# Five of the retention's value projections moved from the recurrences into the RWKV projections

## The chip, the cores and the metric

The kernel runs on one core of a Trainium2 chip. The metric is the device time of one execution in microseconds; several executions are taken and their median is the number that is compared.

## The reference, cut to what matters

One decoder block on 1024 tokens of width 1024, in float32. The normalised input goes through one wide projection whose columns feed two token mixers (RWKV-7 and a chunked retention) and two gates; the mixers' outputs are merged, projected, normalised, and a gated convolutional FFN follows.

```python
hn = rms_norm(h, norm_mix_pre[l])
p = hn @ w_in[l]
p_rw, p_ret, g_rw, g_ret = _split(p, IN_SIZES)
y_rw = rwkv7_mixer(p_rw, ...)
y_ret = retention_mixer(p_ret, positions)      # q, k (rotated), v, g; chunks of 128 tokens
merged = (jax.nn.sigmoid(g_rw) * (y_rw @ w_branch_rw[l])
          + jax.nn.sigmoid(g_ret) * (y_ret @ w_branch_ret[l]))
h = h + rms_norm(merged @ w_out[l], norm_mix_post[l])
f = conv_ffn(rms_norm(h, norm_ffn_pre[l]), ...)
h = h + rms_norm(f, norm_ffn_post[l])
```

## The kernel before

Everything is kept transposed: 128 channels on the partitions, tokens along the free axis. The columns of `w_in` are 54 tiles of 128: tiles 0 to 13 are the RWKV projections, 14 to 21 the retention's queries and keys, 22 to 29 its values, 30 to 37 its gate, 38 to 53 the two merge gates. A float32 product is made of three float32r products (`mm3`, lines 199 to 201: high by high, high by low, low by high), so a tile of 128 columns costs, for each half of 512 tokens, 8 times 3 matmuls of 512 columns: 24 rows on PE. `load_w` (line 178) fetches a weight tile on SP's queue, casts the high part on ACT (line 188) and subtracts the low part on DVE or POOL in turn (line 193).

The stages that matter, in the order of the code:

- **RWKV projections** (`rw_tiles`, line 316, and the loop `for i in range(4)`, line 379). Four tiles first, then for each i the decay and rate products `p_lw` and `p_a`, a long chain on DVE, ACT and POOL that makes the recurrence's operands, and the k, r and v tiles of that i. Their product tiles are called `ps_rw`; `p_sb` are the head sums.
- **RWKV recurrence** (line 553), eight chunks.
- **Side tiles**: `qk_pair` (line 481) and `side_tile` (line 509). A side tile projects one of the tiles 22 to 53, copies it out of PSUM (`ps_side`, two buffers of pool psA, shared with `ps_rw` and `ps_b0`) into `ot`, and writes it to the HBM array `pj_d` on ACT's queue. They stand in the code behind the recurrence (lines 741 to 744) and behind the retention (line 849).
- **Retention** (`first_stage` line 754, `second_stage` line 801), eight chunks. A chunk's data `zvg` comes from `pj_d` in one transfer of 1.5 MB into one of two buffers; a buffer is free again when the chunk's last operation, `yr` (line 840), has read it. First stage: transposes `p_v`, `p_k`, products `p_s`, and `vt`, `sm`, the state `R`. Second stage: `p_o`, its statistics (`rst`, `rmv`), an inverse square root of 14 small DVE operations ending in `nb`, eight activations `on` on ACT, transposes `p_y`, the product `yr`, a write to `yret_d`.
- **Merge**: `ps_b0` (line 871), eight products of 12 rows that need the recurrence's output alone, each taken out of PSUM by a DVE operation on `gt0` (line 873); then the products with the retention's output, whose operand is loaded (`yt`, line 950, ACT's queue), cast (`y_hi`, line 955) and subtracted (`y_lo`, line 956).

The order on each engine isn't the code's: a scheduler places every instruction by a simulated timeline, earlier code having priority, so that work that stands behind fills what it takes for gaps. At run time each engine goes through its list in order.

Of the kernel before, what the change touches and what calls it, by code (L numbers as in the profile page):

```python
# [9 lines left out]
F32 = mybir.dt.float32  # L10
# [8 lines left out]
T = 1024  # L19
# [125 lines left out]
def body(tc, nc, xT, xN, pos, wch, wbrw, wbret, wout, wup, wdn, w2a2, gw2, rows, vecs, consts0, consts1, out):  # L145
    V, S, G, PE = nc.vector, nc.scalar, nc.gpsimd, nc.tensor
    ctx = ExitStack()
    with ctx:
# [147 lines left out]


# [5 lines left out]
        with pctx, tc.tile_pool(name="p1", bufs=1, reuse_waits="tile", side="right") as p1:  # L303
# [57 lines left out]
            rt, rg, k0, r0 = rw_tiles([(12, "v_"), (13, "cs"), (4, "k_"), (0, "r_")], w0)  # L361
            nc.sync.dma_start(cst[1], consts1)
# [16 lines left out]
            for i in range(4):  # L379
# [58 lines left out]
                for c in range(2):  # L438

                    o = 2048 + 128 * i + 64 * (1 - c)  # L440
                    nc.scalar.dma_start(L_d[:, :, o:o + 64].rearrange("j p t -> p j t"), v_.rearrange(jct, c=2, t=64)[:, :, c, :])

# [34 lines left out]


        pj_d = dp.tile([40, 128, T], F32, name="pj_d")

        def qk_pair(m):

            ws = [load_w(wch[14 + 2 * m + e], 8) for e in range(2)]
            for hf in range(2):
                h_ = slice(hf * 512, (hf + 1) * 512)
                ab = []
                for e in range(2):
                    ps = psA.tile([128, 512], F32, tag="a", name="ps_side")
                    proj(ws[e], ps, hf)
                    with tc.high_priority(offset=WPRIO):  # L490
                        t = gp.tile([128, 512], F32, tag=f"qk{e}", name="qk", bufs=1)
                        S.copy(t, ps)
                    ab.append(t)
                a_, b_ = ab
                o1 = gp.tile([128, 512], F32, tag="ot", name="ot")
                t2 = gp.tile([128, 512], F32, tag="rt", name="rot", bufs=1)
                G.tensor_tensor(out=o1, in0=a_, in1=cosT[:, h_], op=ALU.mult)
                V.tensor_tensor(out=t2, in0=b_, in1=sinT[:, h_], op=ALU.mult)
                V.tensor_tensor(out=o1, in0=o1, in1=t2, op=ALU.subtract)
                G.tensor_tensor(out=a_, in0=a_, in1=sinT[:, h_], op=ALU.mult)  # L500
                V.tensor_tensor(out=b_, in0=b_, in1=cosT[:, h_], op=ALU.mult)
                o2 = gp.tile([128, 512], F32, tag="ot", name="ot")
                V.tensor_tensor(out=o2, in0=b_, in1=a_, op=ALU.add)
                dst = pj_d[2 * m:2 * m + 2, :, h_].rearrange("i (e z d) t -> z (i e) d t", e=2, z=2)
                for z, o in enumerate((o1, o2)):
                    for n in range(4):
                        nc.scalar.dma_start(dst[z, n], o[32 * n:32 * n + 32, :])

        def side_tile(i):

            w = load_w(wch[i], 8)
            for hf in range(2):
                ps = psA.tile([128, 512], F32, tag="a", name="ps_side")
                proj(w, ps, hf)
                with tc.high_priority(offset=WPRIO):
                    ot = gp.tile([128, 512], F32, tag="ot", name="ot")
                    if i < 30:
                        S.copy(ot, ps)
                    elif i < 38:
                        V.tensor_tensor(out=ps, in0=ps, in1=rbh(hf), op=ALU.mult)  # L520
                        S.activation(ot, ps, AF.Tanh, scale=0.5)
# [221 lines left out]
        for i in range(22, 38):  # L743
            side_tile(i)
# [535 lines left out]
```

## Time and profile before

| | us |
|---|---|
| three runs | 1914.69, 1915.49, 1908.49 (median 1914.69) |
| the profiled execution | 1908.72 |
| its span, first to last instruction | 1906.9 |
| PE busy in the span | 1802.6 |
| DVE busy in the span | 1194.9 |

The rows further down come from the profiled execution. Times are from the span's start; PE is the matmul engine, PEld its weight loads, DVE, ACT and POOL the elementwise engines, SP the engine that only issues transfers. A row of the timeline has start, length, engine, line, operation, tiles and count, and in brackets how long the engine stood idle before it and what ended that. Granted clock is a share of 2.4 GHz; it has two levels, 1.00 and 0.50, and a value between is a mix of them over the stretch.

### The profile page before, as it was taken

What the parts mean: (1) busy time and instruction counts of PE and PEld (TensorE: products, weight loads), DVE (VectorE), ACT (ScalarE), POOL (GpSimd) and SP (SyncE); (2) the same over time, 40 slices, a digit from 0 to 9 for tenths busy, and PEclk for the clock granted to TensorE, in tenths of its full rate; (3) what the DMA queues carried; (4) which work ended last, traced back from release to release, by engine and by line L of the source; (5) the groups of instructions that cost most, each with busy time, mean ns of one, the idle gap of its engine ahead of it and who ended that gap; (6) DMA issues with size and microseconds to landing.
All of it is one profiled execution on the core that took longest, in us unless ns stands there. A gap on an engine that the chain in (4) does not pass through costs nothing.

```text
span 1906.9 us, 27401 instructions
## 1 busy us (share of the span) xinstructions
PE 1802.6 (95%) x10610; PEld 1450.0 (76%) x10610; DVE 1194.9 (63%) x2052; ACT 648.3 (34%) x993; POOL 700.6 (37%) x506
## 2 busy tenths in 40 slices
PE   8779999999999999999999999888999999999996
PEld 7657778788777788878788777666777777777885
DVE  4786585755666635662545728879888887753413
ACT  6543212111111122332343334543444444543320
POOL 1344523312212221011564734745455455223523
PEclk9989999999999999999999999899999999999998
DMA  8333632433333226554653726343222222774531
GB/s 287 92 105 100 191 82 67 133 90 102 101 105 99 73 93 184 148 169 153 227 155 122 246 80 198 127 139 99 81 75 78 78 78 78 223 212 144 180 92 44
DMA packets 202690, 244.44 MB, mean 128 GB/s; under 512 B 60992, under 2 KB 136256, under 8 KB 201536
## 3 DMA queue, kind: packets, MB, share of 16 engines
q1 hardware_dynamic: 125712, 171.11, 29.7%
q10 hardware_dynamic: 76848, 71.59, 11.5%
q8 instruction: 83, 1.36, 0.3%
q14 instruction: 47, 0.39, 0.1%
HBM read 177.10 MB, written 65.54 MB: 127 GB/s over the span
## 4 chain that ended last, share of the span: by engine, by line
PE 48%; DVE 17%; DMA 9%; issue 4%; POOL 3%; ACT 3%; ACTq 0%; SPq 0%; DVEq 0%; POOLq 0%
PE ps_side L199 6%; PE ps_side L200 6%; PE ps_side L201 6%; DVE u_f L1036 4%; PE ps_dn L201 3%; PE ps_dn L200 3%; PE ps_dn L199 3%; POOL w_lo L1130 2%; DMA w_st<-in_wup_dram 2%; DVE u_f L1038 2%; DVE w_sa L1134 2%; DVE w_sa L1133 2%; PE ps_o L200 1%; PE ps_o L201 1%; PE ps_o L199 1%
## 5 line engine op out<-in xcount | busy, mean ns | idle before, releaser
L193 POOL TENSOR_TENSOR w_lo<-w_st,w_hi 128x1024 fp32r<-128x1024 f32 (+2 forms) x107 | 253.4, 2369 | 495.5 <-PE ps_side L201 167.0
L188 ACT CAST w_hi<-w_st 128x1024 fp32r<-128x1024 f32 (+2 forms) x162 | 161.6, 998 | 406.4 <-PE ps_side L200 129.6
L200 PE MATMUL ps_side<-hnl,w_hi 128*128 128x512 f32 x640 | 255.8, 400 | 0.0
L199 PE MATMUL ps_side<-hnh,w_hi 128*128 128x512 f32 x640 | 255.2, 399 | 0.0
L201 PE MATMUL ps_side<-hnh,w_lo 128*128 128x512 f32 x640 | 254.5, 398 | 0.0
L199 PEld LDWEIGHTS ps_side<-hnh,w_hi 128*128 128x128 f32 x640 | 120.8, 189 | 26.8 <-issue 1.5
L200 PEld LDWEIGHTS ps_side<-hnl,w_hi 128*128 128x128 f32 x640 | 120.7, 189 | 26.3 <-issue 1.5
L201 PEld LDWEIGHTS ps_side<-hnh,w_lo 128*128 128x128 f32 x640 | 120.8, 189 | 26.1 <-issue 0.8
L193 DVE TENSOR_TENSOR w_lo<-w_st,w_hi 128x1024 fp32r<-128x1024 f32 (+1 forms) x55 | 72.2, 1313 | 87.3 <-ACT w_hi L188 50.2
L1036 DVE SCALAR_TENSOR_TENSOR u_f<-ub,vct,u_f 128x512 f32<-128x512 f32 x88 | 104.1, 1187 | 10.0 <-ACT u_f L1035 9.9
L1130 POOL TENSOR_TENSOR w_lo<-w_st,w_hi 128x512 fp32r<-128x512 f32 (+1 forms) x53 | 106.2, 2029 | 0.1
L1035 ACT ACTIVATE u_f<-ub,vct 128x512 f32<-128x512 f32 x76 | 60.0, 813 | 124.0 <-DVE ub L1168 102.4
L199 PE MATMUL ps_rw<-hnh,w_hi 128*128 128x512 f32 (+1 forms) x224 | 87.3, 390 | 13.3 <-ACT hnh L264 7.3
L200 PE MATMUL ps_rw<-hnl,w_hi 128*128 128x512 f32 (+1 forms) x224 | 86.3, 385 | 0.1
L201 PE MATMUL ps_rw<-hnh,w_lo 128*128 128x512 f32 (+1 forms) x208 | 79.9, 384 | 0.0
L201 PE MATMUL ps_b<-y_hi,w_lo 128*128 128x512 f32 x192 | 76.3, 398 | 2.8 <-DVE w_lo L193 2.1
L199 PE MATMUL ps_b<-y_hi,w_hi 128*128 128x512 f32 x192 | 76.2, 397 | 0.9 <-ACT w_hi L188 0.9
L200 PE MATMUL ps_b<-y_lo,w_hi 128*128 128x512 f32 x192 | 76.0, 396 | 0.0
L201 PE MATMUL ps_dn<-f_k,w_lo 128*128 128x512 f32 (+1 forms) x198 | 73.0, 369 | 0.0
L199 PE MATMUL ps_dn<-f_k,w_hi 128*128 128x512 f32 (+1 forms) x198 | 72.9, 368 | 0.0
L200 PE MATMUL ps_dn<-f_k,w_hi 128*128 128x512 f32 (+1 forms) x198 | 72.7, 368 | 0.0
L1038 DVE SCALAR_TENSOR_TENSOR u_f<-ub,vct,u_f 128x512 f32<-128x512 f32 x88 | 71.7, 832 | 0.2
(418 smaller groups left out, 4387.2 us busy)
## 6 DMA issues: line engine op xcount, KB each, us to landing
w_st<-in_wup_dram SPq DMA_DIRECT2D x54, 512.0 KB, 3.6
w_st<-in_wch_dram SPq DMA_DIRECT2D x52, 512.0 KB, 4.0
w_st<-in_wdn_dram SPq DMA_DIRECT2D x38, 512.0 KB, 4.2
pj_d<-ot ACTq DMA_DIRECT2D x64, 256.0 KB, 2.2
zvg<-pj_d SPq DMA_DIRECT2D x8, 1536.0 KB, 9.3
f_d<-u_f ACTq DMA_DIRECT2D x44, 256.0 KB, 2.1
L<-L_d SPq DMA_DIRECT2D x8, 1344.0 KB, 5.9
gt<-pj_d SPq DMA_DIRECT2D x32, 256.0 KB, 4.3
```

The costliest lines, as they stand in the source:

```text
L188: S.copy(hi, st)
L193: eng.tensor_tensor(out=lo, in0=st, in1=hi, op=ALU.subtract)
L199: PE.matmul(ps, wh, xh, start=first and a == 0, stop=False, skip_group_check=skip)
L200: PE.matmul(ps, wh, xl, start=False, stop=False, skip_group_check=skip)
L201: PE.matmul(ps, wl, xh, start=False, stop=last and a == n - 1, skip_group_check=skip)
L1035: S.activation(u, src, AF.Identity, bias=VC("cb")[:, i:i + 1], scale=VC("cw2")[:, i:i + 1])
L1036: V.scalar_tensor_tensor(out=u, in0=ub[:, 1:513], scalar=VC("cw1")[:, i:i + 1], in1=u, op0=ALU.mult, op1=ALU.add)
L1038: V.scalar_tensor_tensor(out=u, in0=ub[:, 0:512], scalar=VC("cw0")[:, i:i + 1], in1=u, op0=ALU.mult, op1=ALU.add)
L1130: eng.tensor_tensor(out=w[1][:, ks, :], in0=src, in1=w[0][:, ks, :], op=ALU.subtract)
L1133: V.tensor_tensor(out=sa[:, lh, :], in0=st2[:, lh, :], in1=st2[:, rh_, :], op=ALU.add)
L1134: V.tensor_tensor(out=sa[:, rh_, :], in0=st1[:, lh, :], in1=st2[:, lh, :], op=ALU.subtract)
```

## The change

`qk_pair`, `side_tile` and the array `pj_d` are moved up in the code, unchanged. Side tiles 22 and 23 are called right behind the first four RWKV tiles, and tiles 24, 25 and 26 at the end of the iterations i = 0, 1 and 2 of the projection loop. The call behind the recurrence begins at tile 27. No operation is added or taken away.

```diff
+        pj_d = dp.tile([40, 128, T], F32, name="pj_d")
+        def qk_pair(m):
...
+        def side_tile(i):
+            w = load_w(wch[i], 8)
+            for hf in range(2):
+                ps = psA.tile([128, 512], F32, tag="a", name="ps_side")
+                proj(w, ps, hf)
+                with tc.high_priority(offset=WPRIO):
+                    ot = gp.tile([128, 512], F32, tag="ot", name="ot")
+                    if i < 30:
+                        S.copy(ot, ps)
...
+                    nc.scalar.dma_start(pj_d[i - 14, :, hf * 512:(hf + 1) * 512], ot)
...
             rt, rg, k0, r0 = rw_tiles([(12, "v_"), (13, "cs"), (4, "k_"), (0, "r_")], w0)
+
+            for i in range(22, 24):
+                side_tile(i)
             nc.sync.dma_start(cst[1], consts1)
...
                     nc.scalar.dma_start(L_d[:, :, o:o + 64].rearrange("j p t -> p j t"), v_.rearrange(jct, c=2, t=64)[:, :, c, :])
+                if i < 3:
+                    side_tile(24 + i)
...
-        for i in range(22, 38):
+        for i in range(27, 38):
             side_tile(i)
```

On PE in the RWKV projections, around the first products with the decay weights (`p_a`, `p_lw`), before:

```order
L201 MATMUL ps_rw<-hnh_0_106,w_lo 128x512
L391 MATMUL p_a<-LA,wlh 128x512
L392 MATMUL p_a<-LA,wll 128x512
L387 MATMUL p_lw<-LW,wlh 128x512
L388 MATMUL p_lw<-LW,wll 128x512
L199 MATMUL ps_rw<-hnh_1_80,w_hi 128x512
```

and now:

```order
L201 MATMUL ps_side<-hnh_0_106,w_lo 128x512
L444 MATMUL p_a<-LA,wlh 128x512
L445 MATMUL p_a<-LA,wll 128x512
L440 MATMUL p_lw<-LW,wlh 128x512
L441 MATMUL p_lw<-LW,wll 128x512
L199 MATMUL ps_side<-hnh_1_80,w_hi 128x512
```

Where rows of the v tile (`ps_rw`) stood, the first side tile stands; in all, 240 side rows now stand among the 568 rows that the projections have behind their first seven half tiles.

On PE at the retention's last chunk (`p_y` are its last transposes), before:

```order
L199 MATMUL ps_side<-hnh_0_82,w_hi 128x512
L839 MATMUL p_y<-cst_69,on 128x128 x2
L200 MATMUL ps_side<-hnl_0_83,w_hi 128x512
L839 MATMUL p_y<-cst_69,on 128x128
L201 MATMUL ps_side<-hnh_0_82,w_lo 128x512
L839 MATMUL p_y<-cst_69,on 128x128 x2
L199 MATMUL ps_side<-hnh_0_86,w_hi 128x512
```

and now, with the rows of the last two chunks:

```order
L796 MATMUL p_R<-vt,kt__6912 64x128 x8
L821 MATMUL p_o<-vt,sm 128x128
L773 MATMUL p_v<-cst_69,zvg 128x128 x4
L782 MATMUL p_s<-zvg 128x128 x8
L773 MATMUL p_v<-cst_69,zvg 128x128 x4
L817 MATMUL p_o<-R,zvg 128x128 x8
L844 MATMUL p_y<-cst_69,on 128x128 x8
L821 MATMUL p_o<-vt,sm 128x128 x8
L844 MATMUL p_y<-cst_69,on 128x128 x8
L199 MATMUL ps_b_8300<-y_hi,w_hi 128x512
```

Before, side rows ran through all eight chunks and 136 of them stood behind the last `p_y`; now the last side row stands in the first stage of chunk 4 (they are counted from 0), two of the eight `ps_b0` products (18 rows up to the `p_y` of chunk 4, 6 behind it) follow there, and the third, `ps_b_8300`, stands behind the last `p_y`.

On DVE at the same place (`gt_8254` takes the first `ps_b0` product out of PSUM), before:

```order
L829 SCALAR_TENSOR_TENSOR nb<-rmv,rh 128x8
L524 TENSOR_TENSOR ot<-ps_side,rbT 128x512
L840 TENSOR_TENSOR yr<-p_y,zvg 128x4x128 x2
L524 TENSOR_TENSOR ot<-ps_side,rbT 128x512 x2
L193 TENSOR_TENSOR w_lo<-w_st,w_hi 128x1024
L524 TENSOR_TENSOR ot<-ps_side,rbT 128x512 x4
L193 TENSOR_TENSOR w_lo<-w_st,w_hi 128x512
L873 SCALAR_TENSOR_TENSOR gt_8254<-gt_8254,ps_b_8256 128x512
```

and now:

```order
L834 SCALAR_TENSOR_TENSOR nb<-rmv,rh 128x8
L845 TENSOR_TENSOR yr<-p_y,zvg 128x4x128 x2
L961 TENSOR_TENSOR y_lo<-yt,y_hi 128x512 x4
L878 SCALAR_TENSOR_TENSOR gt_8254<-gt_8254,ps_b_8256 128x512
L878 SCALAR_TENSOR_TENSOR gt_8276<-gt_8276,ps_b_8278 128x512
L878 SCALAR_TENSOR_TENSOR gt_8298<-gt_8298,ps_b_8300 128x512
```

The four subtractions of the retention's operand now stand ahead of the operation that frees the first `ps_b0` product's bank. From the fifth product with the retention's output on, PE's rows are the same as before.

## Rows read from the trace of the kernel before

**Rows 1.** The page: busy time by engine, and shares of the last chain

```profile
PE 1802.6 (95%) x10610; PEld 1450.0 (76%) x10610; DVE 1194.9 (63%) x2052; ACT 648.3 (34%) x993; POOL 700.6 (37%) x506
PE 48%; DVE 17%; DMA 9%; issue 4%; POOL 3%; ACT 3%; ACTq 0%; SPq 0%; DVEq 0%; POOLq 0%
```

**Rows 2.** Busy time of each engine by stage, with granted clock (PEclk)

```profile
core 0: us, PE busy (x) PEld busy (x) DVE busy (x) ACT busy (x) POOL busy (x), PEclk, DMA share, GB/s
57.50:213.00 155.50, 138.27 (x569) 107.09 (x570) 114.58 (x103) 67.56 (x82) 72.33 (x65) 0.93 0.35 107
350.00:700.00 350.00, 348.69 (x3392) 279.13 (x3391) 206.20 (x576) 62.34 (x99) 65.45 (x65) 1.00 0.32 94
824.00:874.00 50.00, 49.72 (x322) 40.69 (x321) 29.52 (x112) 15.73 (x34) 6.86 (x4) 1.00 0.48 143
904.00:932.50 28.50, 24.74 (x98) 18.69 (x97) 12.93 (x15) 10.81 (x18) 12.87 (x9) 0.94 0.70 229
```

**Rows 3.** The same view, slices of 5 us in the projections

```profile
95.00:100.00 5.00, 1.22 (x2) 0.50 (x2) 4.86 (x3) 0.69 (x1) 4.90 (x4) 0.50 0.22 75
100.00:105.00 5.00, 1.73 (x4) 1.45 (x5) 3.50 (x4) 3.42 (x5) 0.29 (x2) 0.50 0.74 253
105.00:110.00 5.00, 5.00 (x16) 3.87 (x16) 4.55 (x4) 3.10 (x4) 2.19 (x1) 0.65 0.17 61
```

**Rows 4.** Timeline of PE in the projections: waits, and rows at the lower clock

```profile
57.52 0.79 PE L199 MATMUL ps_rw<-hnh,w_x 128*128 128x512 f32 x1 [5.04 <-DVE v__309 L339]
59.39 0.63 PE L200 MATMUL ps_rw<-hnl,w_x 128*128 128x512 f32 x1
59.81 0.63 PE L201 MATMUL ps_rw<-hnh,w_x 128*128 128x512 f32 x1
98.44 0.80 PE L391 MATMUL p_a<-LA,wlh 128*128 128x512 f32 x1 [7.29 <-ACT ta L393]
103.27 0.79 PE L387 MATMUL p_lw<-LW,wlh 128*128 128x512 f32 x1 [3.60 <-ACT th L389]
```

**Rows 5.** Timeline of DVE: side tiles leave PSUM, 24 rows apart

```profile
893.22 0.69 DVE L524 TENSOR_TENSOR ot<-ps_side,rbT 128x512 f32<-128x512 f32 x1 [4.75 <-PE ps_side L201]
898.66 0.69 DVE L524 TENSOR_TENSOR ot<-ps_side,rbT 128x512 f32<-128x512 f32 x1 [4.75 <-PE ps_side L201]
```

**Rows 6.** Timelines of SP and PE: transfers of chunks 6 and 7, and their first user

```profile
823.80 0.36 SPq L760 DMA_DIRECT2D zvg<-pj_d  x1
841.38 0.36 SPq L760 DMA_DIRECT2D zvg<-pj_d  x1
850.30 0.63 PE L768 MATMUL p_v<-cst,zvg 128*128 128x128 f32 x4 [0.28 <-DMA zvg<-pj_d]
```

**Rows 7.** Timelines of DVE, ACT and PE: pieces of a retention chunk

```profile
850.86 1.16 PE L777 MATMUL p_s<-zvg 64*128 64x128 f32 x16
851.05 2.90 ACT L833 ACTIVATE on<-p_o,nb,rh 128x128 f32<-128x128 f32 x8 [4.24 <-DVE nb L829]
859.77 0.89 DVE L820 BATCH_NORM_STATS2 rst<-p_o 128x6 f32<-128x128 f32 x4 [1.32 <-PE p_o L816]
862.03 0.17 DVE L823 TENSOR_TENSOR rve<-rmv,cst 128x8 f32<-128x8 f32 x1
862.23 0.17 DVE L824 TENSOR_SCALAR rve<-rve 128x8 f32<-128x8 f32 x1
873.19 0.69 DVE L840 TENSOR_TENSOR yr<-p_y,zvg 128x512 f32<-128x512 f32 x1 [0.21 <-PE p_y L839]
```

**Rows 8.** Timelines of ACT and DVE: the merge's operand loaded, cast, subtracted

```profile
908.84 0.62 ACT L955 CAST y_hi<-yt 128x512 fp32r<-128x512 f32 x1 [3.38 <-DMA yt<-yret_d]
908.85 1.67 ACTq L950 DMA_DIRECT2D yt<-yret_d  x3
912.15 1.08 DVE L956 TENSOR_TENSOR y_lo<-yt,y_hi 128x512 fp32r<-128x512 f32 x1 [1.81 <-ACT y_hi L955]
932.69 0.69 DVE L873 SCALAR_TENSOR_TENSOR gt<-gt,ps_b 128x512 f32<-128x512 f32 x1 [0.98 <-PE ps_b L201]
```

More of the change, by code (lines that the diff above doesn't have):

```diff
@@ L294, in rbh @@
             return rbT[:, 512 * hf:512 * hf + 512]
+        pj_d = dp.tile([40, 128, T], F32, name="pj_d")
+        def qk_pair(m):
+            ws = [load_w(wch[14 + 2 * m + e], 8) for e in range(2)]
+            for hf in range(2):
+                h_ = slice(hf * 512, (hf + 1) * 512)
+                ab = []
+                for e in range(2):
+                    ps = psA.tile([128, 512], F32, tag="a", name="ps_side")
+                    proj(ws[e], ps, hf)
+                    with tc.high_priority(offset=WPRIO):
+                        t = gp.tile([128, 512], F32, tag=f"qk{e}", name="qk", bufs=1)
+                        S.copy(t, ps)
+                    ab.append(t)
+                a_, b_ = ab
+                o1 = gp.tile([128, 512], F32, tag="ot", name="ot")
+                t2 = gp.tile([128, 512], F32, tag="rt", name="rot", bufs=1)
+                G.tensor_tensor(out=o1, in0=a_, in1=cosT[:, h_], op=ALU.mult)
+                V.tensor_tensor(out=t2, in0=b_, in1=sinT[:, h_], op=ALU.mult)
+                V.tensor_tensor(out=o1, in0=o1, in1=t2, op=ALU.subtract)
+                G.tensor_tensor(out=a_, in0=a_, in1=sinT[:, h_], op=ALU.mult)
+                V.tensor_tensor(out=b_, in0=b_, in1=cosT[:, h_], op=ALU.mult)
+                o2 = gp.tile([128, 512], F32, tag="ot", name="ot")
+                V.tensor_tensor(out=o2, in0=b_, in1=a_, op=ALU.add)
+                dst = pj_d[2 * m:2 * m + 2, :, h_].rearrange("i (e z d) t -> z (i e) d t", e=2, z=2)
+                for z, o in enumerate((o1, o2)):
+                    for n in range(4):
+                        nc.scalar.dma_start(dst[z, n], o[32 * n:32 * n + 32, :])
@@ new lines, in side_tile @@
+        def side_tile(i):
+            w = load_w(wch[i], 8)
+            for hf in range(2):
+                ps = psA.tile([128, 512], F32, tag="a", name="ps_side")
+                proj(w, ps, hf)
+                with tc.high_priority(offset=WPRIO):
+                    ot = gp.tile([128, 512], F32, tag="ot", name="ot")
+                    if i < 30:
+                        S.copy(ot, ps)
+                    elif i < 38:
+                        V.tensor_tensor(out=ps, in0=ps, in1=rbh(hf), op=ALU.mult)
+                        S.activation(ot, ps, AF.Tanh, scale=0.5)
+                        V.scalar_tensor_tensor(out=ot, in0=ot, scalar=1.0, in1=ps, op0=ALU.add, op1=ALU.mult)
+                    else:
+                        V.tensor_tensor(out=ot, in0=ps, in1=rbh(hf), op=ALU.mult)
+                        S.activation(ot, ot, AF.Tanh, scale=0.5)
+                    nc.scalar.dma_start(pj_d[i - 14, :, hf * 512:(hf + 1) * 512], ot)
@@ L476, in body @@
                 V.tensor_tensor(out=dst, in0=dst, in1=rbT, op=ALU.mult)
[L479 to L521, printed above, removed]
-                        V.scalar_tensor_tensor(out=ot, in0=ot, scalar=1.0, in1=ps, op0=ALU.add, op1=ALU.mult)
-                    else:
-                        V.tensor_tensor(out=ot, in0=ps, in1=rbh(hf), op=ALU.mult)
-                        S.activation(ot, ot, AF.Tanh, scale=0.5)
-                    nc.scalar.dma_start(pj_d[i - 14, :, hf * 512:(hf + 1) * 512], ot)
```

## Prediction

> **What bounds the kernel now.** I read the page first: PE is busy 95% of the span and DVE 63% [rows 1], so time is won only where PE stands idle or runs at its lower clock. The busy times by stage say where that is [rows 2]. In the recurrences (350 to 700 us) PE is busy 348.69 of 350 us at clock 1.00; in the retention's end (824 to 874 us) 49.72 of 50. Side tiles fill both. In the RWKV projections (57.5 to 213 us) PE is busy 138.27 of 155.5 us, so 17.2 us idle, at a mean clock of 0.93, with DVE busy 114.58 us. The slices of 5 us show the largest hole [rows 3]: between 95 and 105 us PE is busy 3 of 10 us at clock 0.50 while DVE works nearly throughout, and the clock is back at 1.00 only within the next slice. The timeline names the waits [rows 4]: 7.29 us for ACT's `ta`, whose buffer the DVE chain holds, and 3.60 us for `th`. So the change puts independent matmuls where they fit; the question is what is missing where they were taken away. A side matmul's price is the distance of two evacuations, 898.66 - 893.22 = 5.44 us for 24 rows, 0.227 us a row [rows 5]. At the lower clock it is 59.81 - 59.39 = 0.42 us [rows 4].
>
> **How the sum is made.** The matmuls are the same, only their order differs. I take the stretch from 57.5 us to the end of `ps_b0` at 932.5 us, since the order is nearly the same outside it, and count in it what PE loses against 0.227 us a row or the retention's own pace. The change in that loss is the change in time.
>
> **Gain 1: the projections.** 568 rows at 0.227 us are 128.9 us; they take 155.5 [rows 2], so 26.6 us are lost. What stays: 1.4 us, since the first seven rows run at 0.42 us a row behind a wait of 5.04 us ahead of the first side row [rows 4]; some 3 us between instructions of different shapes (my estimate, from the 26.6 less 17.2 idle less some 6 of the lower clock); and 2 us of waits that I expect to remain. The moved tiles are 240 rows, 54.5 us: the two tiles in front give 21.8 us before the chain's slow part ends, tile 24 another 10.9 around it. I take 20 us as gained; the stage ends at about 213 + 54.5 - 20 = 247 us. The upper end is 25 us (all but the 1.4). The lower end is 8 us: DVE at its 114.58 busy us plus the chain's waits may still set the pace of an iteration. What else moves with the tiles, five weight transfers on SP, five casts, ten copies and ten writes on ACT, five subtractions on DVE or POOL, lies on ACT and POOL at 67.56 and 72.33 us of 155.5 [rows 2]. I cost it at nothing: the cover is their idle time; without it a late cast would stop PE by up to its own length, 0.62 us for half a tile [rows 8].
>
> **Gain 2: `ps_b0`.** Its 96 rows are 21.8 us of work and take 28.5 at clock 0.94 [rows 2]; 6.7 us are lost to weights not yet split. Now most of these weights are loaded during the retention. I take 6, bounds 3 and 6.7.
>
> **Loss 1: chunks 5 to 7 of the retention without cover.** Before, `yr` of chunk 4 ends when the transfer of chunk 6 is issued, 823.8 us [rows 6], and `yr` of chunk 7 at 873.9 [rows 7]: 50 us, of which 125 side rows (counted in the order) are 28.4 and the retention itself some 21.5. Now only 6 rows of `ps_b0` (1.4 us) are left to fill them. The pace is then a chain. The transfer for chunk j+2 waits for `yr` of chunk j and needs 850.30 - 841.38 = 8.9 us to its first user [rows 6]. From `yr` of chunk 4: 9.0 for the transfer; `p_v`, `p_s` and the seven DVE rows up to `nb` of chunk 5, which in the new DVE order stand behind chunk 6's `vt` and `sm`, 4.6 (0.63 and 1.16 on PE, then some 0.7 each for the four wide ones on DVE) [rows 6, 7]; eight `on` with their start 3.2, and `p_y` and `yr` behind the last 1.9 [rows 7]: 18.7 us. From there to `yr` of chunk 7: transfer 9.0; `p_v`, `p_s`, `p_v`, `p_o`, `p_y`, `p_o` on PE 5.3; statistics of chunk 7, 2.1, and 14 small operations at 0.20 us, 2.8 [rows 7]; `on` 3.2; `p_y` and `yr` 1.3: 23.7. Together 42.4 us, of which 21.5 + 1.4 are work: 19.5 us idle. If only DVE's own work set the pace, 29.52 us for three chunks [rows 2] and the last chunk's tail of 7.5 behind it make 37 and 14 idle; that is the lower end. The upper end is 24, with transfers one third slower.
>
> **Loss 2: behind the last `yr`.** Both buffers of pool psA are taken by the first two `ps_b0` products, so the third waits for the DVE operation on the first, and DVE has four `y_lo` ahead of it. These wait for eight casts on ACT, and ACT issues the loads one after the other between them: ten issues and the write of `yret_d` at some 0.5 us (1.67 us for three), 5.5 us, and eight casts at 0.62, 5.0 us; then the last `y_lo`, 1.1, and `gt`, 0.7 [rows 8]. That is 12.3 us behind the last `on`, 11 behind the last `yr`. Before, side rows ran here. Bounds 6 (loads early, casts out of the way) and 14.
>
> **Loss 3: the clock and the seams.** PE now stands still for several us five times in a row, and behind waits of 5 to 7 us its rows ran at 0.42 us instead of 0.227 [rows 3, 4]. Some 5 us of PE work in the chain at twice its price, the restart of `ps_b0` at 1.5, and 1 us of waiting ahead of `yr` of chunk 4: I take 6.5; bounds 2 (the clock stays up) and 10.
> What a page says on this speaks against the change: by the Trainium skill, "TensorE: Matmul & The Clock Gate", section "HAM oscillation — how this bites in real kernels", a matmul stream cut into short bursts between DMA waits starts each burst at half clock. The trace agrees with the direction, 0.50 behind the wait that ended at 98.44 us [rows 3, 4]. By that rule every burst of chunks 6 and 7 is slow and the term is 10, the time 3.5 us longer.
>
> **The sum.** Gains 20 + 6 = 26; losses 19.5 + 11 + 6.5 = 37; net 11 us slower. The profiled execution took 1908.7 us, so 1919.7; it lies 6.0 us below the median of the three runs, 1914.7, and against that the forecast is 1925.7 us. A measurement of this kernel can't tell less than about 0.5%, 9.6 us, from no change, so the forecast lies just above what can be seen.
>
> **Rivals.** *Interleaving pays, faster*: the idle time of the projections is filled wholly and the chunks need less than I count. Gains 25 + 6.7, losses at their lower ends 14 + 6 + 2: 9.7 us faster, 1905. It decides from the point where the last chunks lose under 22 us. For it speaks that 26.6 us of loss are visible in the projections; against it that the wait for `zvg` is in the trace even with side tiles as cover [rows 6], and that all lower ends would have to meet.
> The Trainium skill has this as advice, "Perfetto Trace Analysis", section "Optimization Strategy": where the contended engine changes between regimes, interleave them. The trace agrees that the projections are such a regime, DVE busy 114.58 of 155.5 us; the advice doesn't say what the other regime loses.
> *A draw*: the chunks go at DVE's pace (14), the tail takes 8, the clock 3, gains 24: 1 us slower, 1916. For it speaks that DVE is busy only 29.52 of 50 us there [rows 2].
> *The tiles fill nothing*: the projections' pace is DVE's chain, and side rows delay the products that it waits for (the second `p_a` now stands 72 side rows, 16 us, behind the first). It decides where DVE's chain, and not PE, ends an iteration last. Gain 8 + 3, losses 37: 26 us slower, 1941. Against it: DVE is idle for 41 of 155.5 us there [rows 2], and a hole is filled by any row that doesn't depend on the chain.
> That the change does nothing is excluded: the order shows 240 rows moved.
>
> **How the numbers follow.** Forecast 0.56 (its own range 1915 to 1935, two thirds of it over the 0.5%), draw 0.24, faster 0.09, tiles fill nothing 0.11. Slower by over 0.5%: 0.37 + 0.11 = 0.48. Within 0.5%: 0.19 + 0.24 + 0.02 = 0.45. Faster: 0.07. The range leaves out the faster case and most of the worst: 1907 to 1938.
>
> **What would show it.** The projections should end near 247 us with PE idle under 8 us from 57.5 us on, and no hole like that at 95 us; if they end past 255, gain 1 fails. The recurrences should stay as dense as now. From `yr` of chunk 4 to `yr` of chunk 7 should take about 42 us with a wait of PE for `zvg` of several us in chunks 6 and 7; 35 would make the draw. Between the last `p_y` and `ps_b0` PE should wait some 10 us for DVE's `gt`, with four `y_lo` just before it. Slices at 0.50 should appear in the retention's end. The prediction is wrong if the side tiles' share there turns out to have been no cover, that is if the last chunks are finished in the time that their own PE work takes.

## The result, and the profile after

The changed kernel takes 1941.0 us (median of six executions, 1936.3 to 1946.4), the kernel before 1913.65 (six, 1908.2 to 1915.5): ratio 1.0156, 95% interval 1.0138 to 1.0175; slower by 27 us between the medians, 30 by the ratio. The direction was forecast, the size wasn't: 11 us was the sum, 1938 the end of the range.

The page of the changed kernel's profiled execution (1940.33 us) gives the busy time by engine, the row that answers to the first of [rows 1]:

```profile
PE 1814.3 (94%) x10610; PEld 1459.2 (75%) x10610; DVE 1189.4 (61%) x2052; ACT 648.9 (33%) x993; POOL 696.5 (36%) x506
```

The same number of instructions, 12 us more on PE, which fits a mean granted clock of 0.969 in place of 0.980: more rows ran at the lower clock. The busy times by stage, changed kernel first, show where (columns as in [rows 2]). The stretches are: projections (after only, since [rows 2] has them for before), recurrences from the first side row to the last `p_yT`, retention from there to the last `yr`, merge's start up to the first product with the output weights (`ps_o`), and the rest. The changed kernel has five lines, the kernel before the four behind its projections.

```profile
54.60:249.60 195.00, 188.03 (x807) 149.78 (x808) 118.50 (x103) 77.49 (x97) 81.41 (x68) 0.99 0.36 112
249.60:769.60 520.00, 510.43 (x4630) 406.63 (x4629) 302.27 (x803) 95.99 (x149) 122.20 (x114) 0.99 0.35 100
769.60:926.90 157.30, 137.71 (x906) 111.16 (x904) 89.68 (x316) 41.61 (x93) 16.38 (x13) 0.94 0.52 153
926.90:1002.00 75.10, 63.27 (x264) 51.41 (x265) 33.61 (x34) 25.63 (x35) 40.08 (x24) 0.89 0.64 204
1002.00:1930.70 928.70, 871.38 (x3775) 702.26 (x3774) 614.14 (x723) 374.03 (x558) 425.26 (x274) 0.97 0.39 125
```

```profile
212.50:717.30 504.80, 499.93 (x4599) 400.94 (x4598) 300.42 (x792) 94.94 (x148) 121.82 (x114) 0.99 0.35 102
717.30:873.90 156.60, 155.80 (x1022) 127.15 (x1021) 94.96 (x321) 46.09 (x97) 22.19 (x14) 1.00 0.53 160
873.90:976.50 102.60, 98.84 (x422) 79.72 (x421) 43.75 (x42) 33.17 (x47) 45.54 (x27) 0.98 0.62 199
976.50:1899.80 923.30, 866.59 (x3775) 697.11 (x3773) 609.99 (x723) 372.94 (x558) 428.44 (x275) 0.98 0.40 125
```

The projections are filled: PE idle 7 us, clock 0.99. The slices that held the large hole [rows 3] now read:

```profile
95.00:100.00 5.00, 4.25 (x19) 3.19 (x17) 4.49 (x5) 0.96 (x2) 0.00 (x0) 1.00 0.36 129
100.00:105.00 5.00, 4.12 (x17) 2.79 (x18) 3.53 (x3) 3.46 (x6) 3.73 (x4) 1.00 0.47 131
```

The loss that was expected is in the timeline of PE at the retention's end: the transfers of chunks 6 and 7, `on` of the last chunk, then the DVE operation that frees `ps_b0`'s first buffer, with the rows behind it at the lower clock (0.42 us apart, in place of 0.23).

```profile
888.50 1.09 PE L773 MATMUL p_v<-cst,zvg 128*128 128x128 f32 x4 [4.65 <-DMA zvg<-pj_d]
909.85 1.09 PE L773 MATMUL p_v<-cst,zvg 128*128 128x128 f32 x4 [6.67 <-DMA zvg<-pj_d]
923.24 2.92 PE L844 MATMUL p_y<-cst,on 128*128 128x128 f32 x8 [5.07 <-ACT on L838]
938.73 0.80 PE L199 MATMUL ps_b<-y_hi,w_hi 128*128 128x512 f32 x1 [12.58 <-DVE gt L878]
939.32 0.63 PE L200 MATMUL ps_b<-y_lo,w_hi 128*128 128x512 f32 x1
939.74 0.63 PE L201 MATMUL ps_b<-y_hi,w_lo 128*128 128x512 f32 x1
```

The busy time from `yr` of chunk 4 to `yr` of chunk 7 answers to the third of [rows 2]:

```profile
879.00:926.90 47.90, 29.68 (x199) 23.52 (x198) 25.53 (x107) 10.99 (x28) 3.77 (x4) 0.79 0.48 144
```

What wasn't expected are the 520.0 us of the recurrences. They hold more side rows than before (1439 against 1407, counted in the order), but these are worth 7.3 us, not 15.2.

**One table for all runs.** For every kernel below, a stage's loss is its length less 0.227 us for each row of side tiles and of the merge's products that its order has there: what PE spends on the stage's own work, waits and lower clock. "Rows" are those rows. "Rest" is the time from the first `ps_o` to the first of the last additions on DVE, some 8 us ahead of the span's end (in the kernel before 0.7 us ahead of where the stretch shown above ends). The first two lines were each profiled twice.

| kernel | projections end | recurrences: rows, loss | retention: rows, loss | merge's start: loss | rest | ratio to before (interval) |
|---|---|---|---|---|---|---|
| before | 212.5; 210.6 | 1407, 185.4; 186.2 | 377, 71.0; 71.4 | 6.3; 6.8 | 922.6; 926.8 | 1 |
| changed | 249.6; 252.9 | 1439, 193.4; 191.9 | 265, 97.1; 98.1 | 15.2; 15.1 | 928.6; 923.0 | 1.0156 (1.0138 to 1.0175) |
| drop5 | 209.8 | 1394, 191.3 | 310, 85.9 | 12.9 | 912.1 | 0.9785 (0.9761 to 0.9808) |
| two_front | 219.0 | 1402, 193.0 | 386, 72.0 | 11.5 | 930.6 | 0.9991 (0.9971 to 1.0011) |
| loop_three | 236.5 | 1394, 197.8 | 390, 71.0 | 17.2 | 929.1 | 1.0091 (1.0066 to 1.0117) |
| after_no_ylo | 254.2 | 1439, 194.4 | 265, 96.2 | 9.3 | 932.0 | 1.0136 (1.0106 to 1.0167) |
| late_five | 254.3 | 1407, 186.0 | 297, 85.0 | 12.9 | 922.6 | 1.0040 (1.0022 to 1.0058) |
| late_two | 220.8 | 1409, 187.4 | 380, 69.9 | 10.4 | 927.8 | 0.9956 (0.9940 to 0.9972) |
| after_phase | 248.7 | 1394, 191.4 | 310, 82.3 | 15.0 | 922.2 | 1.0044 (1.0022 to 1.0066) |
| after_phase2 | 249.4 | 1418, 192.6 | 286, 87.5 | 15.2 | 922.3 | 1.0088 (1.0068 to 1.0107) |
| before_phase1 | 212.5 | 1407, 186.2 | 377, 71.2 | 5.7 | 918.1 | 0.9935 (0.9914 to 0.9957) |
| before_rec2 | 210.8 | 1442, 189.2 | 390, 74.0 | 5.4 | 926.9 | 1.0032 (1.0013 to 1.0050) |
| after_x5 | 252.2 | 1439, 192.5 | 373, 73.5 | 3.5 | 924.0 | 1.0244 (1.0220 to 1.0268) |
| after_zvg3 | 249.0 | 1438, 191.2 | 242, 112.1 | 22.3 | 933.0 | 1.0245 (1.0221 to 1.0270) |
| late_two_phase1 | 217.5 | 1409, 186.6 | 380, 70.0 | 9.7 | 914.9 | 0.9883 (0.9862 to 0.9904) |

Three columns carry the story. The retention's loss follows the rows that are left for it: 70 to 74 us with 373 or more, 82 to 88 with 286 to 310, 96 to 98 with 265 (the 112 of `after_zvg3`, with 242, come with a third buffer as well). The recurrences' loss is 185.4 to 187.4 wherever their order is the one of the kernel before, wholly or up to chunk 5, and 189 to 198 wherever it was made anew. And the rest scatters between executions of one kernel by 4.2 and 5.6 us.

### The profile page after: what moved, and what is told of

Its sections match the earlier page's. It is cut to its first block, busy times and chain, and to the rows that moved or that the text cites. A ratio compares the mean times of both kernels' runs of the same rounds, so it can differ in the third digit from the quotient of the medians.

```text
span 1938.5 us, 27386 instructions
## 1 busy us (share of the span) xinstructions
PE 1814.3 (94%) x10610; PEld 1459.2 (75%) x10610; DVE 1189.4 (61%) x2052; ACT 648.9 (33%) x993; POOL 696.5 (36%) x506
## 4 chain that ended last, share of the span: by engine, by line
PE 43%; DVE 19%; DMA 10%; issue 4%; POOL 3%; ACT 3%; ACTq 0%; SPq 0%; DVEq 0%; POOLq 0%
PE ps_side L199 5%; PE ps_side L201 5%; PE ps_side L200 5%; DVE u_f L1041 4%; PE ps_dn L201 3%; PE ps_dn L199 3%; PE ps_dn L200 3%; DVE u_f L1043 2%; POOL w_lo L1135 2%; DMA w_st<-in_wup_dram 2%; DVE w_sa L1139 2%; PE ps_o L200 2%; DVE w_sa L1138 1%; PE ps_o L201 1%; PE ps_o L199 1%
## 5 line engine op out<-in xcount | busy, mean ns | idle before, releaser
L201 PE MATMUL ps_side<-hnh,w_lo 128*128 128x512 f32 x640 | 254.3, 397 | 0.2 <-POOL w_lo L193 0.2
L200 PEld LDWEIGHTS ps_side<-hnl,w_hi 128*128 128x128 f32 x640 | 121.1, 189 | 26.4 <-issue 1.4
L199 PE MATMUL ps_b<-y_hi,w_hi 128*128 128x512 f32 x192 | 76.9, 400 | 12.6 <-DVE gt L878 12.6
```

What stands on the lines that cost most here:

```text
L199: PE.matmul(ps, wh, xh, start=first and a == 0, stop=False, skip_group_check=skip)
L200: PE.matmul(ps, wh, xl, start=False, stop=False, skip_group_check=skip)
L201: PE.matmul(ps, wl, xh, start=False, stop=last and a == n - 1, skip_group_check=skip)
```

## Experiments

### The tiles left out, and only some of them moved

The first three runs take the change apart. `drop5` asks what the missing tiles were worth as cover:

```diff
-        for i in range(22, 38):
+        for i in range(27, 38):
             side_tile(i)
+        for i in range(22, 27):
+            nc.sync.dma_start(pj_d[i - 14], cosT)
```

> The kernel before with tiles 22 to 26 not computed at all; their five rows of the array are filled by copies of another table, so the values of the retention are not the reference's. It issues 240 side rows less, 54.5 us of PE work at 0.227 us a row, and has the uncovered end of the retention that the changed kernel has, but no tile in the projections. Cover theory: the missing rows were cover in the retention's end, so most of their time comes back as idle time: 54.5 saved, 6 more behind the retention, and 19.5 + 11 + 6.5 lost, net 23.5 faster than before, about 1890; yr(4) to yr(7) near 48 us, and a wait of about 12 us for gt behind the last p_y. If the recurrences lose density whenever the scheduler makes their order anew (some 8 us in the changed kernel, not foreseen), the stretch from the first side row of the recurrences to the last p_yT also takes 510 us and not 502, and the time is about 1898. If the density is lost only because of the tiles in the projections, the stretch takes 502. Rival, no cover: the tiles are worth their price wherever they stand, 1859.

Measured: 0.9785, 41 us faster, outside all three figures; 1869 us is nearer to the rival's 1859 than to 1890 or 1898, so that the time alone would speak for the rival, and the stages have to decide. The cover part held: the retention loses 85.9 us against 71.0, in a stretch of which PE is idle 8 us and at a clock of 0.95:

```profile
717.50:873.70 156.20, 147.82 (x951) 119.25 (x949) 92.33 (x319) 44.70 (x98) 20.45 (x15) 0.95 0.53 161
```

156.2 us with five tiles less to compute, as long as the 156.6 with them. The density part held too: 191.3 in the recurrences without any tile in the projections, so the tiles in the projections are not its cause. Three things made it faster than expected: 310 rows were left for the retention and not 265 (about 11 us less loss), the merge's start loses 13 and not 15, and the rest took 912 us, 10 to 15 less than in either execution of the kernel before. Two later runs take up the first and the last of these.

`two_front` moves tiles 22 and 23 only (the call in the loop is gone, the tail begins at 24), `loop_three` only 24 to 26.

> Of the five tiles only the two in front, 22 and 23, are moved; 24 to 26 stay behind the recurrences. In the order 36 side rows (8 us) then still stand behind the last p_y, and side rows run through all eight chunks. Cover theory: no loss in chunks 5 to 7 (yr(4) to yr(7) about 50 us with side rows among them), a wait behind the last p_y of at most 4 us in place of 12.6; the projections gain 11 to 14 us, the large hole being in their reach. About 9 us faster than before, 1905, if the recurrences stay dense; 1911 if they lose half of what they lost in the changed kernel. Rival, the tiles fill nothing: the projections end 21.8 us later than before and the time is 1915 to 1918.

> Only the three tiles of the loop, 24 to 26, are moved; 22 and 23 stay behind the recurrences. The last side row then stands just ahead of the last chunk's p_y: chunks 5 and 6 are covered, the last chunk partly, the merge's start not at all. Cover theory: the projections gain 6 to 8, ps_b0 5, the wait behind the last p_y costs 11, the last chunk 5: about 3 us slower than before, 1917; 1923 if the recurrences lose density as in the changed kernel. If the loss is in proportion to the tiles moved, three fifths of 27 us: 1930.

Measured: 0.9991 for `two_front`, no difference (interval 0.9971 to 1.0011), between the forecasts for dense and half-dense recurrences; 1.0091 for `loop_three`, 17 us slower, against 3 to 9 by the cover theory and 16 by proportion. In `two_front` the retention is covered (loss 72.0) and the projections gain 21.8 - 7.4 = 14.4 us, nearly what all five tiles gain (below), but the recurrences lose 7 us. In `loop_three` the retention is covered as well, better than expected, but the recurrences lose 12 and the wait at the merge's start is all there; the rows of PE behind the last `p_y`, `two_front` first:

```profile
909.82 0.79 PE L199 MATMUL ps_b<-y_hi,w_hi 128*128 128x512 f32 x1 [3.96 <-ACT w_hi L188]
```

```profile
927.20 0.77 PE L199 MATMUL ps_b<-y_hi,w_hi 128*128 128x512 f32 x1 [13.96 <-DVE gt L876]
```

So 36 side rows behind the last `p_y` are cover enough to turn 14 us into 4, and the two tiles in front carry nearly the whole gain. The proportion that fits `loop_three` doesn't fit `two_front` (11 us slower by it, no difference measured).

### The order of the recurrences

The one loss that all these kernels have in common sits in the recurrences, whose own instructions the change doesn't touch. `load_w` counts its calls, and the count decides the engine of the low part: `eng = V if cnt[0] % 3 == 0 or cnt[0] < 3 else G`. Five loads ahead of the recurrences shift it by 2 modulo 3, and with other tiles at the head of the queue, the scheduler makes another order (PE's parts from the old one within chunk 0). `late_five` keeps both as they were: it moves the last five tiles of the queue in place of 22 to 26, and corrects the count.

```diff
-            for i in range(22, 24):
+            for i in range(49, 51):
                 side_tile(i)
...
-                    side_tile(24 + i)
+                    side_tile(51 + i)
...
+        cnt[0] += 1
         for m in range(4):
             qk_pair(m)
-        for i in range(27, 38):
+        for i in range(22, 38):
             side_tile(i)
...
-        for i in range(38, 54):
+        for i in range(38, 49):
             side_tile(i)
+        cnt[0] += -1
```

> As the changed kernel, but the five tiles in the projections are the last ones of the queue, 49 to 53, and 22 to 26 stay behind the recurrences; the counter by which load_w chooses engine and buffers (its value modulo 3) is moved by one ahead of the recurrences and back behind the last side tile. So the side tiles of the recurrences are the same, with the same engines, as in the kernel before, and PE's order there is the same word for word up to chunk 5. The retention's end is as uncovered as in the changed kernel. If the 8 us that the recurrences lost came from the order made anew (other tiles, whose evacuations load DVE at other places, and w_lo on other engines), the stretch from the first side row to the last p_yT takes 505 us, as before, and the time falls from 1941 by 8 to about 1933. If the loss came from what the projections leave behind, the stretch takes 511 or more and the time stays at 1941. Against both: a merge gate's evacuation needs a DVE operation (0.69 us, ten in all) in the projections, which can cost up to 5 us there.

Measured: 1.0040, 7 us slower than before, where the changed kernel is 27 slower. The recurrences take 505.3 us, idle 5.4, as before. Its stretches of recurrences and retention:

```profile
254.30:759.60 505.30, 499.94 (x4598) 400.76 (x4597) 299.33 (x791) 94.82 (x148) 120.89 (x114) 0.99 0.35 102
759.60:912.10 152.50, 142.83 (x938) 115.59 (x936) 91.20 (x317) 42.57 (x95) 19.49 (x15) 0.95 0.53 162
```

More came back than the 8 us foreseen: since the recurrences take 32 rows less, the retention has 32 more, and its loss falls from 97 to 85. `after_phase` and `after_phase2` leave the changed kernel's tiles as they are and correct the count alone, by 1 (to the value that it has before) and by 2 (to the third value); both take the correction back behind the last side tile.

> The changed kernel with load_w's counter moved by one ahead of the recurrences and back behind the last side tile: the recurrences' w_lo are on the engines where the kernel before has them, but the tiles are still 27 and on. PE's order in the recurrences is then that of drop5, which lost 6 us there against 8. If the order alone decides, the stretch takes 508 us for 58.1 half tiles, some 2 us better for its rows than in the changed kernel; time about 1939.

> The changed kernel with load_w's counter moved by two (not one, as in after_phase) ahead of the recurrences and back behind the last side tile: the third value modulo 3. In its order the recurrences take 1418 side rows and leave 262 for the retention, between the 241 of the changed kernel and the 286 of after_phase. If the rows left decide, the retention loses some 18 to 20 us against before, between 11 and 26, and the time lies near 1928. If the changed kernel's value is a bad one for another reason, no order between the three is to be expected.

Measured: 1.0044 and 1.0088. A correction of the count, which changes no arithmetic, takes 20 us of the 27 away. `after_phase`'s expectation had the recurrences right (507.8 us, loss 191.4) and missed the time by 20 us, because it priced the recurrences and forgot what they leave: 1394 rows taken in place of 1439 leave 45 more for the retention, whose loss falls by 15 us. Their own loss hardly fell (192.7 to 191.4): with other tiles at the head of the queue the order is still another one, whatever the count. `after_phase2` was then forecast from the rows left, at 1928, and took 1927.5. Of the three counts the changed kernel drew the one that takes the most rows.

`before_rec2` does the reverse: no tile moved, the count shifted by two as the change does it.

> The kernel before, no tile moved, only load_w's counter moved by two ahead of the recurrences' side tiles and back behind the last side tile, as five moved tiles do it (5 is 2 modulo 3). The order of PE in the recurrences becomes another one, in chunk 0 the same as in the changed kernel. If the recurrences lost density because of this counter, the stretch from the first side row to the last p_yT grows from 505 us by 8 for its 35 rows more and by some 6 to 8 beyond them, to 519 to 521, and the time by the 6 to 8 alone, since 88 side rows are still left as cover behind the last p_y: 1918. If the loss needs the moved tiles, 513 us and 1911.

Measured: 1.0032, 6 us slower, with 516.5 us in the recurrences. 3.4 us of loss appear there and 3 in the retention, so that the stretch lies between the two forecasts, 513 and 519 to 521, and the loss below 6 to 8; with 88 side rows behind the last `p_y`, the merge's start loses nothing. So this shift of the count costs about 6 us where there is cover to spare, and about 20 in the changed kernel, where there isn't.

Where the order costs time shows in part in PE's waits: PE is idle 9.6 us of the changed kernel's recurrences and 4.9 of those before, which is two thirds of the loss. The waits over 1 us in the changed kernel's first profile, three in chunk 0 and one in chunk 2, then the only one in the kernel before:

```profile
276.78 0.68 PE L585 MATMUL p_G<-L 64*128 64x128 f32 x4 [1.47 <-DVE Gm L591]
320.61 0.75 PE L636 MATMUL p_X<-XD,W 32*32 32x32 f32 x64 [1.70 <-DVE W L630]
328.19 0.69 PE L646 MATMUL p_W<-X,Tt 32*32 32x32 f32 x32 [1.14 <-DVE X L638]
430.25 0.75 PE L629 MATMUL p_W<-X,Tt 32*32 32x32 f32 x64 [1.81 <-DVE X L621]
```

```profile
280.72 0.75 PE L624 MATMUL p_W<-X,Tt 32*32 32x32 f32 x64 [1.98 <-DVE X L616]
```

`late_five` has the same wait of 1.98 us in chunk 0; behind it, no wait in either kernel is over 0.8 us. They are links of a chain between DVE and PE. What moves it is not shown: the orders differ in the rows between the links, and in which weights DVE or POOL subtracts, and when.

### Cover restored, and the merge's start

`after_x5` gives the changed kernel its cover back by adding work that nothing needs.

```diff
         for i in range(38, 54):
             side_tile(i)
+        for i in range(5):
+            side_tile(22 + i, to=40 + i)
+        cnt[0] += 1
```

> The changed kernel with five more side tiles behind tile 53, which compute 22 to 26 once more into five added rows of the array (240 rows, 54.5 us of PE work that nothing needs). The recurrences keep the changed kernel's order; the retention's end and the merge's start have side rows again, 108 of them behind the last p_y. Cover theory: chunks 5 to 7 lose nothing (26 us) and the rows behind the last p_y hide the wait for gt and the weights (9 us): the added work costs 54.5 - 35 = 20 us, 1961. If the retention's end were not short of cover, the whole 54.5: 1995.

Measured: 1.0244, 47 us over the kernel before where the changed one is 27 to 30 over it: 17 to 20 us for 54.5 us of added work, so that about 35 us of it were free. Retention and merge's start, the rows to hold against the changed kernel's above:

```profile
771.40:929.60 158.20, 156.01 (x1018) 126.68 (x1017) 92.60 (x316) 45.90 (x97) 19.29 (x12) 1.00 0.53 158
929.60:1023.00 93.40, 91.14 (x395) 73.32 (x394) 35.72 (x36) 31.93 (x46) 47.24 (x28) 1.00 0.66 209
```

The retention takes 158 us as before, with 108 rows more, and the clock is 1.00 throughout. Its loss is 24 us less than in the changed kernel and that of the merge's start 12 less, which is the 35 us. This settles what the side tiles were there: cover.

`after_no_ylo` takes the wait of 12.58 us apart (the `y_lo` of the first half go to POOL, two `gt0` are loaded early into buffers of the side tiles).

```diff
+            with tc.high_priority(offset=WPRIO):
+                g0 = (gp.tile([128, 512], F32, tag="ot", name="g0")
+                      if m < 2 else gt)
+                nc.sync.dma_start(g0, pj_d[24 + m, :, 0:512])
...
-                    (V if i % 2 else G).tensor_tensor(out=lo, in0=yt, in1=hi, op=ALU.subtract)
+                    (V if i % 2 and hf else G).tensor_tensor(out=lo, in0=yt, in1=hi, op=ALU.subtract)
```

> The changed kernel, but the first two gt0 are loaded into free buffers during the retention, their DVE operations have priority, and the y_lo of the first half of tokens go to POOL. PE's order is the same. Nothing then stands between the last yr and the operation that frees ps_b0's first buffer but the space for its result. Tail theory: the wait of 12.6 us behind the last p_y falls to 6 or less, and the time falls by 5 to 8 us, to about 1934. Rival: the products with the retention's output behind it wait instead, for y_lo on POOL or for weights, and the time stays at 1941.

Measured: 1.0136 against 1.0156 and, in a second measurement, 1.0153; the intervals overlap and the medians lie within 1 us of each other against before, so that the 5 to 8 us of the forecast can't be seen in the time, as its rival had it. In the trace the wait falls to 1.38 us and one of 2.51 appears behind it, and the merge's start loses 9.3 us in place of 15.2; the rest took 932.0 us in this execution (its scatter is treated below), which was 5 us slower than the median of the four. The two waits:

```profile
932.30 0.80 PE L199 MATMUL ps_b<-y_hi,w_hi 128*128 128x512 f32 x1 [1.38 <-DVE gt L882]
943.48 0.50 PE L199 MATMUL ps_b<-y_hi,w_hi 128*128 128x512 f32 x1 [2.51 <-DVE gt L882]
```

`after_zvg3` gave the transfers a third buffer (`bufs=3` on `zvg`).

> The changed kernel with three buffers for zvg in place of two, so that a chunk's transfer no longer waits for the yr of the chunk two before. In its order the side rows are used up one chunk earlier. If the transfer is the link that stretches chunks 5 to 7 (PE waits for zvg 4.65 and 6.67 us), these waits go, and last p_yT to last yr, 157 us, falls by about 10; time about 1931. If the chain through DVE's statistics, ACT's on and p_y sets the pace anyway, it stays within 3 us of 157 and the time at 1941.

Measured: 1.0245, 17 to 20 us slower than the changed kernel, which neither forecast had. The wait for `zvg` is still there, the retention loses 112 us for 97 to 98, and the recurrence's output (`yt`), loaded at 748 us in the changed kernel, is loaded only after the last `yr`, at 936 us, so `ps_b0` can't run ahead. SP and PE:

```profile
865.04 26.30 SPq L765 DMA_DIRECT2D zvg<-pj_d  x2
936.43 1.41 SPq L866 DMA_DIRECT2D yt<-yrw_d  x2
```

```profile
900.14 1.12 PE L773 MATMUL p_v<-cst,zvg 128*128 128x128 f32 x4 [7.01 <-DMA zvg<-pj_d]
942.11 1.22 PE L199 MATMUL ps_b<-y_hi,w_hi 128*128 128x512 f32 x2 [9.24 <-ACT y_hi L869]
```

The likely reason is space: `yt` now finds its place only where the retention's buffers were. As a test of the transfer it is inconclusive.

### Two kernels that are faster than both

`late_two` is `late_five` with two tiles (52 and 53, in front; none in the loop). `before_phase1` has one line, `cnt[0] += 1` behind the last side tile of the kernel before. `late_two_phase1` has both.

> Tiles 52 and 53 are moved behind the first four RWKV tiles, nothing into the loop, with the counter's phase kept as in late_five. 35 side rows remain behind the last p_y. If the recurrences' loss comes from their order, two_front without its loss there: 1906.6 less 7.8, about 1899, 0.6% faster than before. If the loss comes from moved tiles as such, 1906.

> The kernel before with load_w's counter moved by one behind the last side tile, as it stands in drop5 modulo 3: the recurrences and the retention are unchanged, and from the merge's weights on, w_lo and the weight buffers fall on other engines and pools. drop5 took 912 us from the first ps_o to the end where the kernel before took 923 for the same work. If that came from this counter, 1900 here; if it was the state in which the stage is entered, 1911 as before.

> late_two with load_w's counter left one further behind the last side tile, as in before_phase1: what late_two gained in the projections (7 to 8 us against before) and what before_phase1 gained behind the retention (12) lie in different stretches. If they add, 1891, 1.0% faster than before; if the merge's start is bound by the same weights in both, no better than before_phase1, 1898.

Measured: 0.9956, 0.9935 and 0.9883; the third is 21 us faster than the kernel before and some 50 faster than the changed one (1888.3 us, five executions). `late_two` missed its forecast by little (1904 for 1899): the projections gained 21.8 - 9.3 = 12.5 us, and the merge's start lost 4. `before_phase1` did what `drop5` had shown. Up to the merge's weights it is the kernel before. Behind them, waits like these of the kernel before, for weights not yet split or for an operation on an engine that splits them, are gone (the first two, in the stage of `ps_o`) or shorter (the third, among the `ps_dn`):

```profile
1093.81 0.50 PE L201 MATMUL ps_o<-m_hi,w_lo 128*128 128x512 f32 x1 [1.30 <-POOL w_lo L193]
1100.18 0.51 PE L200 MATMUL ps_o<-m_lo,w_hi 128*128 128x512 f32 x1 [1.71 <-DVE m_lo L983]
1710.43 0.50 PE L201 MATMUL ps_dn<-f_hl,w_lo 128*128 128x512 f32 x1 [2.23 <-DVE w_lo L193]
```

In that stage (first `ps_o` to first `ps_up`) PE is idle 0.1 us in `before_phase1`, first line, and 4.2 in the kernel before, with 23 rows less in the same length:

```profile
971.90:1135.20 163.30, 163.20 (x728) 133.75 (x726) 94.44 (x113) 64.02 (x96) 89.16 (x52) 1.00 0.50 160
976.50:1140.00 163.50, 159.32 (x705) 129.40 (x704) 85.11 (x109) 61.26 (x92) 85.42 (x49) 1.00 0.48 152
```

### The scatter behind the merge

From the first `ps_o` on, all engines hold the same rows in the same order in both kernels, yet the two profiles differ there by 6.0 us. Both were profiled once more.

> The changed kernel once more, unaltered, for the spread between profiled executions. If the 5 us behind the first ps_o are scatter, this profile shows another length there, anywhere from 922 to 932 us, while the recurrences and the retention repeat within 1 us; the ratio to before repeats at 1.012 to 1.017. If they are a state in which the stage is entered, 928 to 930 again.

> The kernel before once more, unaltered, for the same question: 923 us from the first ps_o to the end if that stage is the same each time, anything from 918 to 930 if it scatters; recurrences 505, retention 156.6.

Measured: ratio 1.0153 (1.0134 to 1.0172) for the changed kernel, and 1912.67 us, a single execution, for the one before. The stretch takes 923.0 us in the changed kernel and 926.8 in the one before, the other way round; changed kernel first:

```profile
1004.70:1927.70 923.00, 865.83 (x3775) 697.25 (x3774) 612.18 (x722) 373.73 (x558) 426.20 (x274) 0.98 0.39 125
```

```profile
976.20:1903.00 926.80, 866.30 (x3775) 696.68 (x3773) 611.18 (x721) 373.61 (x558) 427.07 (x274) 0.98 0.39 125
```

So it is scatter of an execution, and a single profile of this kernel can't carry an argument about less than some 6 us there. The retention repeats within 1.1 us, recurrences and the projections' end within 1.5 and 3.3; of the 3.3, 2.5 arise ahead of the projections' first row (54.6 and 57.1 us).

## Why the prediction was wrong, point by point

With the means of two profiles each, the difference is -14.8 (projections) + 6.9 (recurrences) + 26.4 (retention) + 8.6 (merge's start) + 1.1 (rest) = 28.2 us, against 27.3 and, in the second measurement, 27.6 between the medians. The prediction's sum for the same places was -20, 0, 19.5 + 5 (five of loss 3's 6.5 us), 11 + 1.5 - 6, and 0: 11. Of the 17 us between them 7 are the recurrences, 5 the projections, and 5 the other three together.

- **The step that failed** is the recurrences, put at nothing. "The recurrences should stay as dense as now" stood among the things that would show the prediction right; the sum has no term for them and gives no reason: it calls the order nearly the same outside the stretch from 57.5 to 932.5 us, and the recurrences lie within it. PE's order there was made anew, and they lose 6.9 us more, the largest of the misses. They also take 32 rows more, which the retention then lacks; the prediction had counted the rows that are left, but not seen that the order decides their number. `late_five`, with the same number of tiles in the projections and the old order, is slower than before by 7 us between the medians, where the forecast of 11 would have been in its range. `after_phase`, with the same five tiles and another count, is slower by 7 as well, though there it is the rows left for the retention that differ most.
- **Gain 1** was over-sized: 14.8 us (17.4 in the one pair of profiles, 12.2 in the other) for 20; counted from the stage's own first row it is 14.5 and 12.1, since one execution of the changed kernel began there 3 us early. The term that was too small is the waits that stay: 2 us in the sum, 7 of idle PE in the trace, the largest 2.2 us for DVE. Its place was right, the end of the stage forecast at 247 us and found at 249.6 and 252.9, PE idle 7 us for "under 8". That most of it needs only the tiles in front was not seen: `two_front` has 14.4 of it at two fifths of the lost cover. (The row behind the wait of 5.04 us, called a side row there, is one of `ps_rw`; its price is right.)
- **Gain 2** was 6.1 us for 6: behind the wait and the slow restart, 15.2 - 12.6 - 2.4 = 0.2 us of loss is left in the merge's start, where 6.3 stood before.
- **Loss 1** was right: from `yr` of chunk 4 to `yr` of chunk 7 47.8 us, PE idle 18.2 for 19.5, with the waits for `zvg` in chunks 6 and 7. The 42.4 us were without the clock. (Two transfers one third slower add 6 us and not the 4.5 of the upper end; nothing hangs on it.)
- **Loss 2** had the right size, 12.58 us for 11, and a link too few. DVE's rows there:

```profile
935.76 0.78 DVE L961 TENSOR_TENSOR y_lo<-yt,y_hi 128x512 fp32r<-128x512 f32 x1 [0.89 <-ACT y_hi L960]
937.98 0.69 DVE L878 SCALAR_TENSOR_TENSOR gt<-gt,ps_b 128x512 f32<-128x512 f32 x1 [1.44 <-DMA gt<-pj_d]
```

  `gt` does stand behind the `y_lo`, but at the end it waits for its own load, which SP issued at 931.70 us, 4.8 us behind the last `yr`. By these rows a priority for `gt` alone would have gained nothing; `after_no_ylo` moved the load too.
- **Loss 3** was under-sized. Of the 26.1 us that the retention loses more in the first pair of profiles, 18.8 are idle time (19.6 against 0.8), which leaves 7.3 for the clock and the seams, and 12 rows at 0.42 us behind the wait add 2.4: 9.7 us for 6.5; the term's own pieces, 5 + 1.5 + 1, make 7.5 already. The rule quoted for it from the Trainium skill ("TensorE: Matmul & The Clock Gate", section "HAM oscillation — how this bites in real kernels"), by which each burst between such waits starts slow, made 10 of it; the trace agrees, with a clock of 0.79 from 879 to 926.9 us.
- **The rivals.** *The tiles fill nothing* named 1941 us, the time that was measured, and was wrong in its mechanism: it had 8 us of gain in the projections, and 15 were found. A time that fits does not show a cause. *A draw* needed some 35 us from `yr` to `yr`, and 47.8 were taken. *Interleaving pays* is what `late_two` shows on a smaller scale (0.9956).

What stays open: why every order made anew was worse than that of the kernel before (eleven profiled executions, 189 to 198 us of loss, against 185 to 187 in six with the old order). The trace shows the links, not a rule.

## What to carry to other kernels

Independent work is a budget of cover: before some of it is moved, count what is left for each later stage that leans on it, and with it what the stages between will take. Two tiles at the largest hole brought nearly the gain of five and left the cover in place. And when a helper chooses engines by a running count, any moved or added call re-deals the engines of everything behind it: keep the count when you compare, and try its other values, since here one such shift was worth 20 us in one kernel and 13 in another. Keeping the count does not by itself keep the order: `drop5` and `loop_three` have the old count in the recurrences and lose 6 and 12 us there.

## What the runs showed of the hardware

A small DVE operation can take over ten times its length beside a large one on POOL. In the changed kernel's recurrences DVE multiplies 128x16 elements, two operands from SBUF, in 2.36 us, just while POOL subtracts a weight tile, and 128x24 elements in 0.19 us after it. POOL first, then DVE:

```profile
314.35 2.40 POOL L193 TENSOR_TENSOR w_lo<-w_st,w_hi 128x1024 fp32r<-128x1024 f32 x1
```

```profile
314.42 2.36 DVE L608 TENSOR_TENSOR xprod<-xb,tb 128x16 f32<-128x16 f32 x1 [1.89 <-POOL tb L603]
317.01 0.19 DVE L608 TENSOR_TENSOR xprod<-xb,tb 128x24 f32<-128x24 f32 x1
```

In the recurrences of the kernel before, 8 of the 120 operations `xprod` take over 1.9 us, each begun while POOL runs one of over 1.5 us. Such collisions do not explain the loss of the recurrences: the changed kernel, which loses more there, has 2 of them, the kernel before and `late_five` have 8.

The Trainium skill names a cause for them ("Trainium Architecture — The Big Picture", section "What this means for kernel authors"): DVE and POOL contend for a shared pair of ports to SBUF, which is an exclusive lock and not a split of the bandwidth. The trace agrees.
